# One-bank accumulator tiles for the seven-product pairs, and the two plain pairs finished in the down stage from DRAM

## The chip, the cores and the metric

The kernel runs on one core of a Trainium2 chip. The metric is the device time of one launch in microseconds (us): the median of three runs. A profile of one further execution says where that time goes. Engines are named as the profile names them: PE (TensorE, matmuls) with PEld (its weight loads), DVE (VectorE), ACT (ScalarE), POOL (GpSimd) and SP (SyncE, which here only issues DMAs).

## The reference, cut to what matters

One decoder layer for 1024 tokens of 1024 channels: a token-mixing half (dilated attention, a convolution module, gates) and then the channel-mixing half (FFN), which alone is changed:

```python
h = rms_norm(x, norm_ffn_pre)                         # 1024 x 1024
u = h @ w_up                                          # 1024 x 5632: 22 gate and 22 value columns of 128
u = causal_depthwise_conv(u, ffn_conv_w, ffn_conv_b)  # 3 taps along the tokens
u_gate, u_val = jnp.split(u, 2, axis=-1)
f = gelu(u_gate, approximate=True) * u_val            # 1024 x 2816
y = f @ w_down
x = x + rms_norm(y, norm_ffn_post)
```

All products are carried out in fp32 accuracy as three matmuls each, on operands split into a high part (`wh`, `xh`) and a low part (`wl`, `xl`): high by high, high by low, low by high.

## The kernel before, in words

**Where the FFN stands.** Attention, convolution and output projection come first and are not touched. From about 1125 us on the FFN's up stage computes, for each j from 0 to 21, a gate block and a value block of 128 channels by 1024 tokens. `us` is the name of such blocks in the plain pairs; in the trace all of them, and all other 128 by 1024 work tiles, are called `u` (six buffers).

**PSUM tiles.** There are eight banks of 128 by 512 fp32. `pp` is a tile of two banks with two buffers; `ps` is one bank with two buffers; `pt` and `po` are one bank with one buffer each. Dependencies between instructions are found by the Tile layer, tile by tile.

**The plain pairs** (`up_plain`, j = 0 and 1) do the full eight products of 12 matmuls each per pair: two columns c (gate and value), two token halves h, two halves kh of the inner dimension. Pair 0 sums into two `pp` tiles, one for each c, with the token halves side by side; pair 1 into `ps`, `ps`, `pt` and `po`. Each finished bank is copied to `us` (L731, by ACT for c = 0 and by DVE for c = 1). At the end `up_plain` finishes both pairs: scale and bias on ACT (`scaled`, L680), two taps on DVE (`taps`, L686), gelu on ACT (L736), product on DVE (L737), store to the DRAM buffer `fscr` by a POOL DMA (L738).

**The seven-product pairs** (class `Seven`, j = 2 to 21) need seven products P1 to P7 instead of eight. They use sums of weight quadrants made on POOL (L758) and sums T1 to T4 of the token operands, which DVE, ACT and POOL prepare during `up_plain` (L639, L640, L660 to L671). A pair has two accumulators, b1 and b2. P1, P2 and P3 add into b1, and P5, P6, P7 and P4 into b2; in between, `take` copies partial sums out, or from one accumulator to the other:

- after P5: b2 to the gate block (L774), then b1 over b2 (L775), both ACT
- after P2: b1 to the gate block (L777, ACT); after P6: b2 over b1 (L779, ACT)
- after P7 and P3: DVE adds of b2 (L782) and of b1 (L784) into the value and the gate block
- after P4: b2 to the value block (L786, ACT)

In the kernel before, b1 and b2 are the two banks of one `pp` tile, and successive pairs take its two buffers in turn.

**What sets the order.** For the seven-product pairs a table sets it: `AT` gives each product a place, seven places to a pair, and all steps of all pairs are sorted by place and rank and written out under a manual schedule. So PE runs, round and round, P2 and P6 of pair n, P1 of pair n + 1, P7 of n, P5 of n + 1, P3 and P4 of n. Weights are split (`wsplit`: L166 on ACT, L167 on DVE; seven buffers) five places ahead, scale, taps, gelu (L798), product (L804) and store (L807) of a pair follow at places 13 to 17. `up_plain` and the down stage are ordered by the scheduler, from their place in the code, and each engine works its own list strictly in order.

**The down stage** (`down(0)`, `down(1)`, one for each half of the tokens) loads block k of `fscr` by a POOL DMA (L858), splits it (L859 on ACT, L860 on DVE) and two weight pieces (L166, L167), and adds 24 matmuls into eight banks, two for each of four token tiles t. The last three k are done tile by tile, and `finish` (L838 to L849) normalises and writes a finished tile.

Of the kernel before, what the change touches and what calls it, by code (L numbers as in the profile page):

```python
# [11 lines left out]
F32 = mybir.dt.float32  # L12
# [6 lines left out]
P = 128  # L19
S = 1024  # L20
# [58 lines left out]
def trunk_kernel(ctx: ExitStack, tc: tile.TileContext, a, out):  # L79
# [9 lines left out]
    def pp_tile():  # L89
        return psum.tile([P, S], F32, tag="pp", name="pp", bufs=2)  # L90
# [3 lines left out]
    def ps_tile(shape=(P, 512), tag=None):  # L94

        if tag is None:
            tag = ("ps", "pt", "ps", "po")[banks[0] % 4]
            banks[0] += 1
        return psum.tile(list(shape), F32, tag=tag, name=tag, bufs=2 if tag == "ps" else 1)
# [574 lines left out]

    with tc.tile_pool(name="ffn", bufs=1) as ffn:
        fscr = dram.tile([NF, P, S], F32, name="fscr")

        def scaled(src, c):
            o = u_tile()
            nc.scalar.activation(o, src, AF.Identity, scale=ffn_w[:, c, 2:3], bias=ffn_b[:, c:c + 1])  # L680
            return o

        def taps(o, src, c):
            for k in (1, 0):
                d = 2 - k
                nc.vector.scalar_tensor_tensor(o[:, d:], src[:, :S - d], ffn_w[:, c, k:k + 1], o[:, d:],  # L686
                                               op0=ALU.mult, op1=ALU.add)
# [24 lines left out]
        def up_plain(js):  # L712

            us = {(j, c): u_tile() for j in js for c in range(2)}
            pps = [pp_tile() for c in range(2)]
            kept = {}
            for h in range(2):
                for n, j in enumerate(js):
                    for c in range(2):
                        ps = pps[c][:, h * 512:(h + 1) * 512] if n == 0 else ps_tile(tag=("ps", "ps", "pt", "po")[2 * h + c])  # L720
                        for kh in range(2):
                            key = j, 2 * c + kh
                            if h == 0 or key not in kept:
                                w = wsplit(quadrant(*key))
                                if len(kept) < 7:
                                    kept[key] = w
                            else:
                                w = kept[key]
                            product(ps, w, ("B11", "B21", "B12", "B22")[2 * h + kh], kh == 0, kh == 1)
                        dst = us[j, c][:, h * 512:(h + 1) * 512]  # L730
                        (nc.vector.tensor_copy if c else nc.scalar.copy)(dst, ps)  # L731
            for j in js:
                o = [scaled(us[j, c], c * NF + j) for c in range(2)]
                for c in range(2):
                    taps(o[c], us[j, c], c * NF + j)
                nc.scalar.activation(o[0], o[0], AF.Gelu_apprx_tanh)  # L736
                nc.vector.tensor_mul(o[0], o[0], o[1])  # L737
                nc.gpsimd.dma_start(fscr[j], o[0])  # L738

# [6 lines left out]
        class Seven:  # L748
# [13 lines left out]

            def multiply(self, p):
                if p == "P1":
                    both = pp_tile()
                    self.b1, self.b2 = both[:, 0:512], both[:, 512:1024]
                b = self.b1 if p in ("P1", "P2", "P3") else self.b2
                product(b, self.t[p], OPERAND[p], p in ("P1", "P5"), False, True)

# [81 lines left out]
        def down(h, late=3):  # L851
            wide = [pp_tile() for _ in range(2)]
            banks = [[w[:, cs] for cs in cols] for w in wide]
            banks += [[ps_tile(tag="ps") for _ in range(2)], [ps_tile(tag=tag) for tag in ("pt", "po")]]

            def load(k):
                ft = dt(F32R, (P, 2, 512))
                nc.gpsimd.dma_start(f(ft[:, 1]), fscr[k][:, h * 512:(h + 1) * 512])  # L858
                nc.scalar.copy(ft[:, 0], f(ft[:, 1]))  # L859
                nc.vector.tensor_sub(ft[:, 1], f(ft[:, 1]), f(ft[:, 0]))  # L860
                w = []
                for cs in cols:
                    raw = raw_tile()
                    nc.sync.dma_start(raw, a["w_down"][k * P:(k + 1) * P, cs])
                    w.append(wsplit(raw))
                return ft, w

            def step(t, k, ft, w):
                ts = slice(t * P, (t + 1) * P)
                for q in range(2):  # L870
                    mm3(banks[t][q], ft[:, 0, ts], ft[:, 1, ts], *w[q], k == 0, k == NF - 1)

            order = (3, 2, 0, 1)
            for k in range(NF - late):
                fw = load(k)
                for t in order:
                    step(t, k, *fw)
            fws = [(k, load(k)) for k in range(NF - late, NF)]
            for t in order:
                for k, fw in fws:  # L880
                    step(t, k, *fw)
                finish(4 * h + t, banks[t])
# [71 lines left out]
```

## Time and profile before

| | us |
|---|---|
| median of 3 runs (1868.88 to 1870.09) | 1869.4 |
| the profiled execution, device time | 1867.9 |
| its span, first to last instruction | 1866.1 |
| PE busy (95% of the span) | 1777.1 |
| DVE busy (63%) | 1170.3 |
| ACT busy (38%) | 717.4 |
| POOL busy (11%) | 206.0 |

All times from the trace are of the one profiled execution, counted from the start of its span. 1.8 us of its device time lie outside the span, and the median of the runs is 1.5 us above it. A row of the time line gives start, duration, engine, line, operation, output and inputs, shapes and a count where equal instructions are joined; in brackets stands how long the engine had been idle before, and what released it. Matmul rows overlap: a matmul's row lasts 0.39 us while the next starts after about 0.23. The granted clock is a share of TensorE's full 2.4 GHz, so 0.50 is its lower level, 1.2 GHz.

### The profile page before, as it was taken

Reading aid. Unit: us, or ns where it says so; the run is one execution under the profiler, and the core shown is the slowest. Engines: PE = TensorE matmul, PEld = TensorE weight load, DVE = VectorE, ACT = ScalarE, POOL = GpSimd, SP = SyncE. Lnnn points to the kernel's source line nnn. Section 1 sums busy time; section 2 is a strip of 40 time slices with the busy share of each in tenths; the row PEclk is TensorE's granted clock in tenths of the full one; section 3 lists DMA queues with packets and bytes.
Section 4 is the critical chain, followed back from the end, with each engine's and each line's share of the span. In section 5 each row is a group of like instructions: output and inputs, shape, how many; then the busy total and the mean of one; then the engine's idle time right before and its main releaser. Section 6 shows DMA issues by size and latency. Waiting matters only on the chain.

```text
span 1866.1 us, 22153 instructions
## 1 busy us (share of the span) xinstructions
PE 1777.1 (95%) x8152; PEld 1479.1 (79%) x8152; DVE 1170.3 (63%) x1971; ACT 717.4 (38%) x1327; POOL 206.0 (11%) x233
## 2 busy tenths in 40 slices
PE   7899998999999999999999999899999999999997
PEld 5688898888888888888888887677777777788886
DVE  6249979258762869738645578856655566753524
ACT  6132343233323342223432344545444454642322
POOL 0000010011100000000000002232232222120000
PEclk9899999999999999999999999899999999999999
DMA  5312132112312222344231432322232222573522
GB/s 189 108 49 60 45 97 81 45 58 62 95 52 53 68 68 80 102 172 147 92 112 57 142 108 90 96 91 79 85 98 88 86 79 91 180 249 126 173 93 100
DMA packets 83133, 184.01 MB, mean 99 GB/s; under 512 B 11203, under 2 KB 13139, under 8 KB 83024
## 3 DMA queue, kind: packets, MB, share of 16 engines
q1 hardware_dynamic: 67536, 139.75, 23.8%
q0 software_dynamic: 12240, 39.27, 6.5%
q10 hardware_dynamic: 3248, 3.58, 0.6%
q8 instruction: 64, 1.05, 0.2%
q14 instruction: 45, 0.37, 0.1%
HBM read 147.81 MB, written 36.85 MB: 99 GB/s over the span
## 4 chain that ended last, share of the span: by engine, by line
PE 61%; issue 28%; DVE 4%; POOL 2%; DMA 2%; ACT 1%; ACTq 1%; SPq 0%; POOLq 0%; DVEq 0%
PE pp L709 21%; PE pp L186 10%; PE pp L187 10%; PE pp L188 10%; PE ps L186 1%; PE ps L188 1%; PE ps L187 1%; DVE u L784 1%; ACTq L258 1%; ACT u L777 1%; POOL oscr L416 1%; POOL mscr L416 1%; PE pt L188 1%; PE po L188 1%; PE po L187 1%
## 5 line engine op out<-in xcount | busy, mean ns | idle before, releaser
L186 PE MATMUL pp<-d,wh 128*128 128x512 f32 x1088 | 428.0, 394 | 15.3 <-DVE d L332 15.0
L188 PE MATMUL pp<-d,wl 128*128 128x512 f32 x1088 | 427.4, 393 | 0.0
L187 PE MATMUL pp<-d,wh 128*128 128x512 f32 x1088 | 427.0, 393 | 0.0
L709 PE MATMUL pp<-d,wh 128*128 128x512 f32 x1184 | 375.3, 398 | 41.7 <-DVE u L784 17.0
L271 DVE SCALAR_TENSOR_TENSOR acc<-cin,conv_w,acc 128x1024 f32<-128x1024 f32 x240 | 305.2, 1281 | 3.1
L709 PEld LDWEIGHTS pp<-d,wh 128*128 128x128 f32 x1184 | 221.4, 190 | 104.0 <-DVE u L784 25.1
L186 PEld LDWEIGHTS pp<-d,wh 128*128 128x128 f32 x1088 | 205.1, 189 | 57.8 <-issue 16.0
L188 PEld LDWEIGHTS pp<-d,wl 128*128 128x128 f32 x1088 | 205.0, 188 | 41.3
L187 PEld LDWEIGHTS pp<-d,wh 128*128 128x128 f32 x1088 | 205.2, 189 | 40.8
L709 PE MATMUL pp<-d,wl 128*128 128x512 f32 x592 | 232.8, 393 | 0.0
L167 DVE TENSOR_TENSOR wl<-wr,wh 128x512 fp32r<-128x512 f32 x200 | 136.5, 687 | 152.5 <-ACT wh L166 152.0
L166 ACT CAST wh<-wr 128x512 fp32r<-128x512 f32 x200 | 123.3, 621 | 264.7 <-PE pp L187 166.5
L167 DVE TENSOR_TENSOR wl<-wq,wh 128x512 fp32r<-128x512 f32 x148 | 108.2, 740 | 99.7 <-ACT wh L166 97.1
L166 ACT CAST wh<-wq 128x512 fp32r<-128x512 f32 x148 | 91.1, 623 | 126.9 <-PE pp L188 104.7
L167 DVE TENSOR_TENSOR wl<-ws,wh 128x512 fp32r<-128x512 f32 x80 | 63.2, 790 | 113.1 <-ACT wh L166 113.1
L709 PEld LDWEIGHTS pp<-d,wl 128*128 128x128 f32 x592 | 112.4, 190 | 24.2
L686 DVE SCALAR_TENSOR_TENSOR u<-u,ffn_w 128x1023 f32<-128x1023 f32 x88 | 113.5, 1292 | 3.4 <-ACT u L680 2.0
L186 PE MATMUL pp<-wh,d 128*128 128x512 f32 x232 | 90.1, 391 | 0.7 <-ACT u L616 0.7
L187 PE MATMUL pp<-wl,d 128*128 128x512 f32 x232 | 90.4, 390 | 0.0
L188 PE MATMUL pp<-wh,d 128*128 128x512 f32 x232 | 90.4, 390 | 0.0
L325 PE MATMUL pp<-wh,d 128*128 128x512 f32 x192 | 79.1, 413 | 3.0 <-DVE d L332 3.0
L326 PE MATMUL pp<-wl,d 128*128 128x512 f32 x192 | 78.4, 408 | 0.0
(293 smaller groups left out, 2527.7 us busy)
## 6 DMA issues: line engine op xcount, KB each, us to landing
wq<-in_w_up_dram SPq DMA_DIRECT2D x100, 256.0 KB, 2.7
wq<-in_w_down_dram SPq DMA_DIRECT2D x88, 256.0 KB, 3.1
wr<-in_w_v_dram SPq DMA_DIRECT2D x48, 256.0 KB, 2.8
wr<-in_w_qk_dram SPq DMA_DIRECT2D x48, 256.0 KB, 2.7
fscr<-u POOLq DMA_DIRECT2D x22, 512.0 KB, 2.9
d<-fscr POOLq DMA_DIRECT2D x44, 256.0 KB, 5.2
wr<-in_w_glu_dram SPq DMA_DIRECT2D x32, 256.0 KB, 2.7
wr<-in_w_gate_dram SPq DMA_DIRECT2D x32, 256.0 KB, 2.7
```

The lines of the kernel that those rows point to most:

```text
L166: nc.scalar.copy(hi, raw)
L167: nc.vector.tensor_sub(lo, raw, f(hi))
L186: nc.tensor.matmul(ps, lh, rh, start=first, stop=False)
L187: nc.tensor.matmul(ps, lh, rl, start=False, stop=False)
L188: nc.tensor.matmul(ps, ll, rh, start=False, stop=last)
L258: nc.scalar.dma_start(bscr[4 * g:4 * g + 4, :, :BW[g]], vscr[4 * g:4 * g + 4, BOFF[g]:BOFF[g] + BW[g]].unsqueeze(1).to_broadcast((4, P, BW ...
L271: nc.vector.scalar_tensor_tensor(acc, cin[:, k:k + S], conv_w[:, m, k:k + 1], acc, op0=ALU.mult, op1=ALU.add)
L325: nc.tensor.matmul(ps, hTh[k][:, sl], wh, start=k == 0, stop=False)
L326: nc.tensor.matmul(ps, hTh[k][:, sl], wl, start=False, stop=False)
L416: nc.gpsimd.dma_start(dst[:, r, :, g, j, :], src[:, 2 * r:2 * r + 2, :])
L686: nc.vector.scalar_tensor_tensor(o[:, d:], src[:, :S - d], ffn_w[:, c, k:k + 1], o[:, d:], op0=ALU.mult, op1=ALU.add)
L709: nc.tensor.matmul(ps, wp[:, cs], xp, start=first and k == 0 and n == 0, stop=last and k == 3 and n == 2, skip_group_check=open_)
```

## The change

Two things are changed. First, b1 and b2 of a seven-product pair are two tiles of one bank each: `ps` and `ps` where j is even, `pt` and `po` where it is odd. Second, `up_plain` keeps pair 0 in one `pp` tile for each token half, copies all banks on ACT, after both columns are done, and then stores the raw blocks to a new DRAM buffer `uscr`. Scale, taps, gelu and product of the two plain pairs are a function of their own, `plain_out`, which loads them back. It is called in `down(0)`, after the fifth and the tenth k. So that `fscr[0]` and `fscr[1]` are wanted late, the down stage takes k from 2 to 21 and then 0 and 1, and its token tiles in the order 0 to 3.

```diff
--- before.py
+++ after.py
@@ -674,6 +674,7 @@
 
     with tc.tile_pool(name="ffn", bufs=1) as ffn:
         fscr = dram.tile([NF, P, S], F32, name="fscr")
+        uscr = dram.tile([2, 2, P, S], F32, name="uscr")
 
         def scaled(src, c):
             o = u_tile()
@@ -712,12 +713,15 @@
         def up_plain(js):
 
             us = {(j, c): u_tile() for j in js for c in range(2)}
-            pps = [pp_tile() for c in range(2)]
             kept = {}
             for h in range(2):
                 for n, j in enumerate(js):
-                    for c in range(2):
-                        ps = pps[c][:, h * 512:(h + 1) * 512] if n == 0 else ps_tile(tag=("ps", "ps", "pt", "po")[2 * h + c])
+                    if n == 0:
+                        both = pp_tile()
+                        pss = [both[:, 0:512], both[:, 512:1024]]
+                    else:
+                        pss = [ps_tile(tag=tag) for tag in (("ps", "ps"), ("pt", "po"))[h]]
+                    for c, ps in enumerate(pss):
                         for kh in range(2):
                             key = j, 2 * c + kh
                             if h == 0 or key not in kept:
@@ -727,15 +731,23 @@
                             else:
                                 w = kept[key]
                             product(ps, w, ("B11", "B21", "B12", "B22")[2 * h + kh], kh == 0, kh == 1)
-                        dst = us[j, c][:, h * 512:(h + 1) * 512]
-                        (nc.vector.tensor_copy if c else nc.scalar.copy)(dst, ps)
+                    for c, ps in enumerate(pss):
+                        nc.scalar.copy(us[j, c][:, h * 512:(h + 1) * 512], ps)
             for j in js:
-                o = [scaled(us[j, c], c * NF + j) for c in range(2)]
                 for c in range(2):
-                    taps(o[c], us[j, c], c * NF + j)
-                nc.scalar.activation(o[0], o[0], AF.Gelu_apprx_tanh)
-                nc.vector.tensor_mul(o[0], o[0], o[1])
-                nc.gpsimd.dma_start(fscr[j], o[0])
+                    nc.gpsimd.dma_start(uscr[j, c], us[j, c])
+
+        def plain_out(j):
+
+            o = []
+            for c in range(2):
+                u = u_tile()
+                nc.gpsimd.dma_start(u, uscr[j, c])
+                o.append(scaled(u, c * NF + j))
+                taps(o[c], u, c * NF + j)
+            nc.scalar.activation(o[0], o[0], AF.Gelu_apprx_tanh)
+            nc.vector.tensor_mul(o[0], o[0], o[1])
+            nc.gpsimd.dma_start(fscr[j], o[0])
 
 
 
@@ -762,8 +774,7 @@
 
             def multiply(self, p):
                 if p == "P1":
-                    both = pp_tile()
-                    self.b1, self.b2 = both[:, 0:512], both[:, 512:1024]
+                    self.b1, self.b2 = [ps_tile(tag=tag) for tag in (("ps", "ps"), ("pt", "po"))[self.j % 2]]
                 b = self.b1 if p in ("P1", "P2", "P3") else self.b2
                 product(b, self.t[p], OPERAND[p], p in ("P1", "P5"), False, True)
 
@@ -868,15 +879,17 @@
             def step(t, k, ft, w):
                 ts = slice(t * P, (t + 1) * P)
                 for q in range(2):
-                    mm3(banks[t][q], ft[:, 0, ts], ft[:, 1, ts], *w[q], k == 0, k == NF - 1)
-
-            order = (3, 2, 0, 1)
-            for k in range(NF - late):
+                    mm3(banks[t][q], ft[:, 0, ts], ft[:, 1, ts], *w[q], k == 2, k == 1)
+
+            ks = [*range(2, NF), 0, 1]
+            for n, k in enumerate(ks[:-late]):
                 fw = load(k)
-                for t in order:
+                for t in range(4):
                     step(t, k, *fw)
-            fws = [(k, load(k)) for k in range(NF - late, NF)]
-            for t in order:
+                if h == 0 and n in (4, 9):
+                    plain_out(n // 9)
+            fws = [(k, load(k)) for k in ks[-late:]]
+            for t in range(4):
                 for k, fw in fws:
                     step(t, k, *fw)
                 finish(4 * h + t, banks[t])
```

Three places of the engines' order, before and after (no times are in these rows; a wait is named by the engine or DMA queue whose semaphore is waited for). On PE, in the steady run of the seven-product pairs, the end of P2 and the start of P6 of pair 20. The first is written to b1, the second to b2. Before:

```order
L709 MATMUL pp_12176<-d168_8615,wl_12196 128x512
L709 MATMUL pp_12176<-d169_8616,wh_12195 128x512 x2
L709 MATMUL pp_12176<-d169_8616,wl_12196 128x512
L709 MATMUL pp_12176<-d186_9146,wh_12212 128x512 [waits Activation_49]
L709 MATMUL pp_12176<-d186_9146,wh_12212 128x512
L709 MATMUL pp_12176<-d186_9146,wl_12213 128x512
```

After:

```order
L710 MATMUL ps_12177<-d168_8615,wl_12198 128x512
L710 MATMUL ps_12177<-d169_8616,wh_12197 128x512 x2
L710 MATMUL ps_12177<-d169_8616,wl_12198 128x512
L710 MATMUL ps_12178<-d186_9146,wh_12214 128x512 x2
L710 MATMUL ps_12178<-d186_9146,wl_12215 128x512
L710 MATMUL ps_12178<-d187_9150,wh_12214 128x512 x2
```

P6 stood behind a wait for ACT and has none now; both products, and their place behind each other, are as they were. P4 behind P3 keeps a wait for DVE in both kernels.

On ACT, where the plain pairs end and the first `take` (the copies after P5 of pair 2) stands; the plain pairs' raw blocks are `u_9201` to `u_9204` before and `u_9202` to `u_9205` after (a wait for DMASW is one for a POOL DMA, here the store of `u_9202` to `uscr`). Before:

```order
L680 ACTIVATE u_9465<-u_9201,ffn_b_80,ffn_w_79 128x1024 [waits DVE_49]
L680 ACTIVATE u_9467<-u_9202,ffn_b_80,ffn_w_79 128x1024 [waits DVE_49]
L736 ACT_TABLE_LOAD [waits DVE_49]
L736 ACTIVATE u_9465<-u_9465 128x1024 [waits Activation_49]
L680 ACTIVATE u_9476<-u_9203,ffn_b_80,ffn_w_79 128x1024
L680 ACTIVATE u_9478<-u_9204,ffn_b_80,ffn_w_79 128x1024 [waits DVE_49,Activation_49]
L774 COPY u_9558<-pp_9511 128x512 [waits DVE_49,PE_49]
L775 COPY pp_9511<-pp_9511 128x512 [waits Activation_49]
```

After:

```order
L639 CAST d195_9184<-u_9123 128x512 [waits DVE_49]
L639 CAST d196_9189<-u_9124 128x512 [waits DVE_49]
L735 COPY u_9205<-po_9409 128x512 [waits PE_49]
L639 CAST d197_9194<-u_9124 128x512 [waits DVE_49,Activation_49]
L842 DMA d198_12513<-in_norm_ffn_post_dram 128x1024 [waits Activation_49]
L785 COPY u_9542<-ps_9495 128x512 [waits DMASW5_49,PE_49,Activation_49]
L786 COPY ps_9495<-ps_9494 128x512 [waits Activation_49]
```

The four scalings, the gelu and its table load of the plain pairs are gone from ahead of the first `take`, whose copies now follow the last casts of the operand sums and a bank copy.

On DVE, at the start of the down stage, behind the taps of the last pair, 21 (`u_12497` before, `u_12500` after); `u_12723`, `u_12729` and `u_12938` are blocks of the plain pairs. Before:

```order
L686 SCALAR_TENSOR_TENSOR u_12502<-u_12470,ffn_w_79,u_12502 128x1023 [waits Activation_49]
L686 SCALAR_TENSOR_TENSOR u_12502<-u_12470,ffn_w_79,u_12502 128x1022 [waits DVE_49]
L167 TENSOR_TENSOR wl_12651<-wq_12648,wh_12650 128x512 [waits DMAHW5_49,Activation_49]
L167 TENSOR_TENSOR wl_12685<-wq_12682,wh_12684 128x512 [waits DMAHW6_49,Activation_49]
L167 TENSOR_TENSOR wl_12691<-wq_12688,wh_12690 128x512 [waits DMAHW7_49,Activation_49]
L804 TENSOR_TENSOR u_12497<-u_12497,u_12502 128x1024 [waits DVE_49]
L167 TENSOR_TENSOR wl_12725<-wq_12722,wh_12724 128x512 [waits DMAHW0_49,Activation_49]
L167 TENSOR_TENSOR wl_12731<-wq_12728,wh_12730 128x512 [waits DMAHW2_49,Activation_49]
L167 TENSOR_TENSOR wl_12765<-wq_12762,wh_12764 128x512 [waits DMAHW3_49,Activation_49]
L167 TENSOR_TENSOR wl_12771<-wq_12768,wh_12770 128x512 [waits DMAHW4_49,Activation_49]
```

After:

```order
L815 TENSOR_TENSOR u_12500<-u_12500,u_12505 128x1024 [waits DVE_49]
L687 SCALAR_TENSOR_TENSOR u_12723<-u_12721,ffn_w_79,u_12723 128x1023 [waits DMASW7_49,DMASW5_49,Activation_49]
L167 TENSOR_TENSOR wl_12694<-wq_12691,wh_12693 128x512 [waits DMAHW7_49,Activation_49]
L167 TENSOR_TENSOR wl_12743<-wq_12740,wh_12742 128x512 [waits DMAHW0_49,Activation_49]
L167 TENSOR_TENSOR wl_12749<-wq_12746,wh_12748 128x512 [waits DMAHW1_49,Activation_49]
L167 TENSOR_TENSOR wl_12783<-wq_12780,wh_12782 128x512 [waits DMAHW2_49,Activation_49]
L687 SCALAR_TENSOR_TENSOR u_12723<-u_12721,ffn_w_79,u_12723 128x1022 [waits DVE_49]
L687 SCALAR_TENSOR_TENSOR u_12729<-u_12727,ffn_w_79,u_12729 128x1023 [waits DMASW0_49,Activation_49]
L167 TENSOR_TENSOR wl_12789<-wq_12786,wh_12788 128x512 [waits DMAHW3_49,Activation_49]
L687 SCALAR_TENSOR_TENSOR u_12729<-u_12727,ffn_w_79,u_12729 128x1022 [waits DVE_49]
L687 SCALAR_TENSOR_TENSOR u_12938<-u_12936,ffn_w_79,u_12938 128x1023 [waits DMASW2_49,DMASW1_49,Activation_49]
L749 TENSOR_TENSOR u_12723<-u_12723,u_12729 128x1024 [waits DVE_49,Activation_49]
```

The taps and the product of the plain pairs now stand between the weight splits (L167) of the down stage; ACT's scalings and gelus, and POOL's four loads and two stores, stand likewise among those of the down stage.

## Rows read from the trace of the kernel before

**Rows 1.** Windows: us, busy PE, PEld, DVE, ACT, POOL (count), clock, DMA share, GB/s.
```profile
1125.00:1185.50 60.50, 56.09 (x248) 45.29 (x246) 53.65 (x99) 30.38 (x58) 17.98 (x12) 0.94 0.26 83
...
1214.30:1573.50 359.20, 334.35 (x1428) 265.39 (x1428) 216.12 (x241) 172.62 (x256) 97.35 (x87) 1.00 0.28 88
1573.50:1607.70 34.20, 29.90 (x120) 23.54 (x121) 22.12 (x27) 20.29 (x32) 10.01 (x18) 0.95 0.41 132
...
1627.00:1855.40 228.40, 228.40 (x1008) 188.87 (x1006) 101.50 (x209) 79.13 (x143) 12.84 (x24) 1.00 0.44 145
1855.40:1866.10 10.70, 0.01 (x1) 0.00 (x0) 7.45 (x29) 2.03 (x5) 0.00 (x0) 0.61 0.42 158
```

**Rows 2.** Waits of PE from 1214 to 1574: total us, times, longest.
```profile
PE pp L709 <- DVE u L784: 14.1, 18, 0.8
PE pp L709 <- ACT u L777: 11.5, 17, 0.7
```

**Rows 3.** Time line of PE in one round of the seven-product pairs.
```profile
1541.25 0.62 PE L709 MATMUL pp<-d,wh 128*128 128x512 f32 x2
...
1550.77 0.62 PE L709 MATMUL pp<-d,wh 128*128 128x512 f32 x2
1551.22 0.39 PE L709 MATMUL pp<-d,wl 128*128 128x512 f32 x1
1552.40 0.74 PE L709 MATMUL pp<-d,wh 128*128 128x512 f32 x2 [0.78 <-DVE u L784]
...
1558.85 0.73 PE L709 MATMUL pp<-d,wh 128*128 128x512 f32 x2 [0.68 <-ACT u L777]
```

**Rows 4.** Time lines of DVE (first row) and ACT in the same round.
```profile
1557.24 2.60 DVE L686 SCALAR_TENSOR_TENSOR u<-u,ffn_w 128x1023 f32<-128x1023 f32 x2
...
1558.21 0.58 ACT L777 COPY u<-pp 128x512 f32<-128x512 f32 x1 [0.47 <-PE pp L709]
...
1559.87 1.06 ACT L798 ACTIVATE u<-u 128x1024 f32<-128x1024 f32 x1 [0.56 <-DVE u L686]
1561.96 0.57 ACT L779 COPY pp<-pp 128x512 f32<-128x512 f32 x1 [1.03 <-PE pp L709]
```

**Rows 5.** Time line of PE at the plain pairs and the first seven-product pair.
```profile
1152.65 1.22 PE L709 MATMUL pp<-d,wh 128*128 128x512 f32 x2 [2.97 <-DVE u L731]
...
1193.45 1.22 PE L709 MATMUL pp<-d,wh 128*128 128x512 f32 x2 [8.09 <-ACT pp L775]
...
1194.89 1.05 PE L709 MATMUL pp<-d,wh 128*128 128x512 f32 x2
...
1196.17 1.05 PE L709 MATMUL pp<-d,wh 128*128 128x512 f32 x2
```

**Rows 6.** Time lines of DVE (first row) and ACT behind the plain pairs.
```profile
1183.52 5.10 DVE L686 SCALAR_TENSOR_TENSOR u<-u,ffn_w 128x1023 f32<-128x1023 f32 x4
...
1188.44 2.36 ACT L680 ACTIVATE u<-u,ffn_b,ffn_w 128x1024 f32<-128x1024 f32 x2
1192.21 0.59 ACT L774 COPY u<-pp 128x512 f32<-128x512 f32 x1 [1.41 <-DVE u L737]
```

**Rows 7.** Time lines of POOL, DVE and PE where the down stage's loads begin.
```profile
1583.98 2.58 POOL L858 DMA_DIRECT2D d<-fscr  x4 [8.09 <-PE pp L709]
...
1596.06 0.68 DVE L784 TENSOR_TENSOR u<-pp,u 128x512 f32<-128x512 f32 x1
...
1596.80 0.73 PE L709 MATMUL pp<-d,wh 128*128 128x512 f32 x2 [2.92 <-DVE u L784]
```

**Rows 8.** The page's DMA issues: count, KB each, median us to landing.
```profile
fscr<-u POOLq DMA_DIRECT2D x22, 512.0 KB, 2.9
d<-fscr POOLq DMA_DIRECT2D x44, 256.0 KB, 5.2
```

**Rows 9.** Time lines of ACT and DVE behind the last matmul.
```profile
1855.44 0.58 ACT L838 COPY u<-pp 128x512 f32<-128x512 f32 x1 [1.74 <-PE pp L188]
...
1856.06 0.69 DVE L839 COPY u<-pp 128x512 f32<-128x512 f32 x1
```

## The prediction

> **What bounds the kernel now.** I read the windows by stage first [rows 1]. From 1627.0 to 1855.4 us, in the down stage, PE is busy in all of 228.40 us: 1008 matmuls, 0.2266 us each, and nothing but fewer or faster matmuls could shorten it. The seven-product stretch from 1214.3 to 1573.5 is not like that: 1428 matmuls (17 rounds of 84) take 359.20 us, 0.2515 each, at a granted clock of 1.00. DVE is busy for 60% of it, ACT for 48%, POOL for 27%, so no other engine is the bound. Then I read the list of waits for the same stretch [rows 2]: PE waits for two lines only, 18 times for DVE's L784 and 17 times for ACT's L777, once each in a round. The time line of a round shows them [rows 3]: P4 starts 0.78 us late behind the add that empties b1 after P3, and P6 0.68 us late behind the copy that empties b1 after P2. Both products write b2, the other bank of the same tile. They are waits for a tile, not for data. That is where to look in the rows: the releaser reads a bank that the waiting product does not write.
>
> How fast does a round run where nothing stops it? From 1541.25 to 1550.77 there are 14 groups of three matmuls [rows 3]: 9.52 / 42 = 0.2267 us each, the same as in the down stage. I take it for the rest.
>
> **The change part by part.** All terms are made against the profiled execution, 1867.9 us.
>
> (a) Steady rounds. 1428 x 0.2267 = 323.7 us, so the stretch loses 359.2 - 323.7 = 35.5 us, 2.09 a round. That is more than the listed waits (14.1 + 11.5 = 25.6): a matmul that starts late also gives up its overlap with the one before, as 1551.22 + 0.23 = 1551.45 against 1552.40 shows (0.95 us for a listed 0.78), and the first few after it run a little slower [rows 3]. With a tile for each bank the order's rows have no wait ahead of P6. P4 keeps one for DVE, but what it must wait for is the add after P7 (L782), which reads b2 and stands two products earlier. So the whole 35.5 goes, if nothing else is late. What is late next? P7 writes b2 after the copy L779, which stands on ACT behind the gelu of the pair before, and that behind DVE's taps. In the round shown the gelu ends at 1559.87 + 1.06 = 1560.93 [rows 4]. Without its wait P6 would start at 1558.85 - 0.83 = 1558.02 and end 2.72 later, at 1560.74; the copy takes 0.57 [rows 4], so it is done by about 1561.7 with the passing on. P1 of the next pair runs meanwhile, to 1563.46, and only then is P7 due: 1.8 us to spare. Taken: 35.5, bounds 25 (half a microsecond a round comes back) and 35.5.
>
> *The Trainium skill, page "PSUM — Partial Sum Buffer", section "PSUM bank collisions raise a hardware error", has it that engines must be kept apart by bank (and quarter of the partitions), and that different banks may be used at once. By it, nothing on the chip asks for the waits in rows 2, and the sum is as in (a); were two neighbouring banks barred together, (a) would be 0. No row of before has PE and ACT on the two banks of one pair at once, so the trace doesn't yet say.*
>
> (b) The first pair. In before, P2 of pair 2 starts 8.09 us late [rows 5], since the copies L774 and L775 stand on ACT behind the plain pairs' scalings and gelu, and those behind DVE's taps and product [rows 6]. Then 12 matmuls run at half the clock: 1.28 us for three [rows 5], 0.427 each, which costs 12 x 0.20 = 2.4. With the two ordinary waits of that round (2.09) and 0.2 of overlap, 12.8 us are lost between P5's end and P4. The order shows the scalings and the gelu gone from there. What stays: P2 must wait for the two copies after P5, 0.59 [rows 6] and about 0.57, and some 0.3 for passing on, 1.5 us. The first copy also waits for the store of a raw block to `uscr` to land, since it takes over its buffer; such a store takes 2.9 us [rows 8], its block is copied out some 11 us (pair 1's last products, P1 and P5) before P5 ends, so it is hidden; if it isn't, it costs a few us once. Gain 11.3, bounds 7 and 12.8.
>
> (c) The plain pairs. PE waits 2.97 us for DVE's copy L731 and then runs 12 matmuls at half the clock (2.4) [rows 5]: 5.4 us. Now no copy is on DVE, and the second half goes to another `pp` tile. But DVE's operand sums set the pace there (53.65 of 60.50 us busy [rows 1]), the next operands' casts stand on ACT behind three copies of about 0.5 us, and transposes and short waits stay. Half of it stays, I estimate: gain 2.5, bounds 0 and 5.4.
>
> (d) The end of the pairs. From 1573.5 to 1607.7 120 matmuls take 34.2 us where 27.2 would do [rows 1]: 7.0 lost, in three ordinary waits and one of 2.92 us at P4 of pair 20, behind DVE's L784 [rows 7]. DVE and ACT were held by splits of down-stage blocks, whose loads start at 1583.98 [rows 7] and take 5.2 us to land [rows 8]. In the new order P4 no longer waits for L784, and the add it does wait for ends about a microsecond before P4 is due. But the first down-stage matmuls come earlier, and their weight splits stand on DVE behind the same blocks and the taps of pair 20: I work out from the rows' durations that they are late by some 2 to 3 us, with a few matmuls at half the clock behind. Gain 3.5, bounds 0 and 7.
>
> (e) The end. The last tile is now `pt` and `po`, not one `pp`: DVE's copy need not follow ACT's (1856.06 after 1855.44 + 0.58 [rows 9]). Gain 0.6.
>
> (f) What is added. Four raw stores, four loads, and the finishing of two pairs in the down stage. On DVE that is 8 taps of 1.28 (5.10 / 4 [rows 6]) and 2 products of about 1.2: 12.6 us; on ACT 4 scalings of 1.2 and 2 gelus of 1.06 [rows 4, 6]: 7 us. PE covers it: in its 228.40 us DVE has 127 free and ACT 149 [rows 1], and the weight splits that are queued behind run up to seven buffers, three and a half k (19 us of PE), ahead. A raw block's way is load, scale, taps, gelu, product, store, load: about 5 + 1 + 3 + 1 + 1 + 3 + 5 = 19 us, and blocks 0 and 1 are wanted after 18 others of 5.4 us each. POOL's queue holds only loads and stores by then. Cost 0. If the cover fails at the two places where ACT waits for a raw block, each costs a load's 5 to 6 us: bound 12.
>
> Sum: 35.5 + 11.3 + 2.5 + 3.5 + 0.6 = 53.4, so 1867.9 - 53.4 = 1814.5. The median of the runs lies 1.5 us above the profiled execution: **1816.0**.
>
> **The rivals.** *A new wait in each round.* The 1.8 us to spare at P7 is the smallest I found. If a faster PE makes ACT's line (sums on POOL, split, scale, taps, gelu, copy) late by more, each microsecond beyond it costs 20 us. For it: the chain passes through three engines that work strictly in order. Against it: all three are idle 40% or more of a round, and the chain starts from PE's own products. Half a microsecond to 1.2 a round: 1826 to 1840.
>
> *The change does not do what it says:* the two waits stay, because P4's and P6's partner copies must be over for another reason, a bank rule or a count that the semaphore passes late. Then (a) is nothing, and (b) to (e) leave about 17 us, less the waits in them: 1853. For it: P4 keeps a wait for DVE. Against it: P6 has none for ACT.
>
> *The down stage doesn't cover* the moved work (f): up to 12 us back, 1828.
>
> *Slower:* the clock. Without its pauses PE works on for some 400 us in the pairs; if the chip then granted 1.2 GHz for part of it, each matmul would take 0.427 instead of 0.227 [rows 3, 5]. 268 of the 1680 (16%) would eat the 53.4 us, and half of them at that level would end at 1867.9 - 53.4 + 168 = 1982 us. Against it: 228.40 us without a pause at clock 1.00 [rows 1]; for it, only that the half clock occurs at all, and each time here behind a pause of about 3 us or more [rows 5].
>
> *The Trainium skill, page "TensorE: Matmul & The Clock Gate", Part 1, has the low clock as the default, which activity lifts: by it steady work can't bring this rival about. The trace agrees in rows 1 and 5.*
>
> **How the numbers follow.** The forecast as worked out: 0.82. A new wait in each round 0.08, the waits stay 0.03, the down stage doesn't cover 0.04, the clock 0.03. Within the forecast the bounds of (b) to (d) give at best 35.5 + 12.8 + 5.4 + 7 + 0.6 = 61.3 (1808), and at worst 35.5 + 7 + 0 + 0 + 0.6 = 43.1 (1826). All three at one end at once is unlikely; I take 1809 to 1828, which holds nearly all of the forecast, the down-stage case and the lower edge of the new wait, and leaves out about 0.14. A measurement of this kernel can tell about 0.2% (4 us) from no change. Faster by more than that: 0.96; within it 0.01; slower 0.03.
>
> **What the profile would show.** (a) right: a stretch of 17 rounds takes about 324 us, without a wait ahead of P4 or P6; wrong, if PE waits for L790 (the new copy after P6) or for a split. (b): P2 of the first pair waits 1 to 2 us, not 8. (c): no wait for a copy among the plain pairs, but small ones for operands. (d): some 2 to 3 us of waiting for a split where the down stage starts. (f): PE without a pause from there to its end; a wait there for L166, L167 or L870 would show the moved work uncovered. The forecast is wrong as a whole if rounds still take over 20 us.

## The result, and the profile after

The changed kernel takes 1818.4 us (median of four runs, 1814.4 to 1822.7), the kernel before 1869.7 (1868.9 to 1870.3). The ratio is 0.9726, with a 95% interval of 0.9703 to 0.975: 51 us saved. Forecast were 1816.0 and a range of 1809 to 1828. The profiled execution of the changed kernel is the longest of its four: 1822.7, with a span of 1820.6.

The first thing to read is where the FFN begins, since nothing ahead of it was changed. The rows of L616, a copy in the output projection some 70 us ahead of it, give count, shortest, median and longest duration in ns, then the first and the last start. Before:

```profile
L616 ACT COPY u<-pp x14: 585/590/608, 1054.5 to 1114.6; 128x512 f32<-128x512 f32 x14
```

After:

```profile
L616 ACT COPY u<-pp x14: 587/591/609, 1061.1 to 1121.2; 128x512 f32<-128x512 f32 x14
```

The same work comes 6.6 us later in the profiled execution of after. So the stretches must be set side by side from there, not by their times. Windows of after (us, then busy PE, PEld, DVE, ACT and POOL with counts, granted clock, DMA share, GB/s):

```profile
1131.60:1188.35 56.75, 53.29 (x248) 43.41 (x246) 48.33 (x93) 30.50 (x60) 23.39 (x15) 1.00 0.30 98
1188.35:1206.05 17.70, 16.43 (x72) 13.63 (x73) 7.55 (x9) 8.32 (x15) 7.22 (x6) 1.00 0.53 164
1206.05:1529.75 323.70, 323.70 (x1429) 268.02 (x1428) 228.92 (x241) 175.50 (x259) 99.59 (x88) 1.00 0.33 100
1529.75:1556.95 27.20, 27.20 (x121) 22.34 (x119) 20.08 (x25) 18.71 (x29) 10.94 (x18) 1.00 0.49 155
1556.95:1580.10 23.15, 21.36 (x87) 17.15 (x86) 18.35 (x25) 12.02 (x20) 2.48 (x5) 0.93 0.58 195
1580.10:1808.50 228.40, 228.40 (x1008) 188.81 (x1006) 111.18 (x220) 84.97 (x148) 16.07 (x30) 1.00 0.47 157
1808.50:1820.60 12.10, 0.01 (x1) 0.00 (x0) 8.22 (x29) 1.92 (x5) 0.00 (x0) 0.58 0.55 188
```

[rows 1] holds the answering rows of before for five of these; two stretches of before were not among them:

```profile
1185.50:1214.35 28.85, 19.41 (x72) 14.98 (x72) 21.13 (x22) 15.09 (x23) 9.76 (x9) 0.82 0.30 101
...
1607.70:1627.00 19.30, 19.30 (x87) 15.96 (x86) 14.47 (x22) 9.60 (x16) 2.49 (x5) 1.00 0.68 225
```

| stretch | before | after | change | forecast |
|---|---|---|---|---|
| up to the first copy of L616 | 1054.5 | 1061.1 | +6.6 | 0 |
| plain pairs, to the end of P5 (c) | 60.5 | 56.8 | -3.7 | -2.5 |
| first pair, to its P4 (b) | 28.9 | 17.7 | -11.2 | -11.3 |
| 17 steady rounds (a) | 359.2 | 323.7 | -35.5 | -35.5 |
| end of the pairs and start of the down stage (d) | 34.2 + 19.3 | 27.2 + 23.2 | -3.1 | -3.5 |
| rest of the down stage, with the added work (f) | 228.4 | 228.4 | 0.0 | 0 |
| behind the last matmul (e) | 10.7 | 12.1 | +1.4 | -0.6 |

The whole list of PE's waits in the changed part (us, times, longest) has three rows now, where [rows 2] alone held 35 waits:

```profile
PE pp L710 <- DVE d L640: 3.4, 2, 2.3
PE pp L187 <- DVE wl L167: 1.8, 1, 1.8
PE ps L710 <- ACT ps L786: 1.3, 1, 1.3
```

One steady round of after, first PE's rows where P6 and P7 start (start, duration, engine, line, operation, tiles, shape, count), then ACT's:

```profile
1420.96 0.62 PE L710 MATMUL ps<-d,wh 128*128 128x512 f32 x2
...
1426.40 0.62 PE L710 MATMUL ps<-d,wh 128*128 128x512 f32 x2
```

```profile
1421.16 0.59 ACT L788 COPY u<-ps 128x512 f32<-128x512 f32 x1 [0.47 <-PE ps L710]
...
1422.82 1.06 ACT L809 ACTIVATE u<-u 128x1024 f32<-128x1024 f32 x1 [0.55 <-DVE u L687]
1423.93 0.57 ACT L790 COPY ps<-ps 128x512 f32<-128x512 f32 x1
```

P6 begins at 1420.96, right behind P2, while ACT copies b1 from 1421.16 to 1421.75. In [rows 3, 4] P6 began only when that copy was over. L790, on which P7 depends, ends at 1423.93 + 0.57 = 1424.50, and P7 is due at 1426.40: 1.9 us to spare, 1.8 were forecast.

*The Trainium skill, page "PSUM — Partial Sum Buffer", section "PSUM bank collisions raise a hardware error", lets two engines use different banks at once. The trace agrees here: P6 writes one ps bank in the 0.59 us in which ACT reads the other, and its matmuls keep their step.*

Where the down stage starts, PE's rows and then DVE's:

```profile
1559.96 0.50 PE L187 MATMUL pp<-wl,d 128*128 128x512 f32 x1 [1.79 <-DVE wl L167]
...
1561.99 0.63 PE L188 MATMUL ps<-wh,d 128*128 128x512 f32 x1
```

```profile
1554.91 2.60 DVE L687 SCALAR_TENSOR_TENSOR u<-u,ffn_w 128x1023 f32<-128x1023 f32 x2
...
1558.03 1.28 DVE L687 SCALAR_TENSOR_TENSOR u<-u,ffn_w 128x1023 f32<-128x1023 f32 x1
1559.22 1.89 DVE L167 TENSOR_TENSOR wl<-wq,wh 128x512 fp32r<-128x512 f32 x3
```

The split for which PE waits stands behind the taps of pair 20, as forecast, and 1.6 us behind the pause eight matmuls run at 0.427 us each, the half clock (1.2 GHz). Both together make most of the 3.9 us that this start costs in this execution.

### The profile page after: what moved, and what is told of

Read it like the earlier page. It is cut to its first block, busy times and chain, and to the rows that moved or that the text cites. A ratio compares the mean times of both kernels' runs of the same rounds, so it can differ in the third digit from the quotient of the medians.

```text
span 1820.6 us, 22184 instructions
## 1 busy us (share of the span) xinstructions
PE 1767.3 (97%) x8152; PEld 1483.4 (81%) x8152; DVE 1177.1 (65%) x1967; ACT 720.7 (40%) x1331; POOL 215.4 (12%) x241
## 4 chain that ended last, share of the span: by engine, by line
PE 61%; issue 29%; DVE 3%; POOL 3%; DMA 2%; ACT 1%; ACTq 1%; SPq 0%; POOLq 0%; DVEq 0%
PE ps L710 10%; PE pp L186 10%; PE pp L187 10%; PE pp L188 10%; PE po L710 6%; PE pt L710 4%; PE ps L188 1%; PE ps L187 1%; PE ps L186 1%; PE pp L710 1%; POOL oscr L416 1%; ACTq L258 1%; POOL mscr L416 1%; PE po L188 1%; PE pt L188 1%
## 5 line engine op out<-in xcount | busy, mean ns | idle before, releaser
L186 PE MATMUL pp<-d,wh 128*128 128x512 f32 x1088 | 430.0, 396 | 15.1 <-DVE d L332 14.8
L188 PE MATMUL pp<-d,wl 128*128 128x512 f32 x1088 | 428.9, 394 | 0.0
L187 PE MATMUL pp<-d,wh 128*128 128x512 f32 x1088 | 428.7, 394 | 0.0
L186 PEld LDWEIGHTS pp<-d,wh 128*128 128x128 f32 x1088 | 206.2, 189 | 58.0 <-issue 15.7
L188 PEld LDWEIGHTS pp<-d,wl 128*128 128x128 f32 x1088 | 206.1, 189 | 41.7
L187 PEld LDWEIGHTS pp<-d,wh 128*128 128x128 f32 x1088 | 206.3, 190 | 41.2
L167 DVE TENSOR_TENSOR wl<-wr,wh 128x512 fp32r<-128x512 f32 x200 | 136.9, 689 | 153.8 <-ACT wh L166 152.7
L710 PE MATMUL ps<-d,wh 128*128 128x512 f32 x592 | 182.6, 389 | 1.3 <-ACT ps L786 1.3
L167 DVE TENSOR_TENSOR wl<-wq,wh 128x512 fp32r<-128x512 f32 x148 | 119.3, 814 | 93.5 <-ACT wh L166 93.5
L710 PEld LDWEIGHTS ps<-d,wh 128*128 128x128 f32 x592 | 111.1, 188 | 24.8 <-ACT ps L786 1.7
L167 DVE TENSOR_TENSOR wl<-ws,wh 128x512 fp32r<-128x512 f32 x80 | 63.7, 799 | 81.6 <-ACT wh L166 81.6
L710 PE MATMUL ps<-d,wl 128*128 128x512 f32 x296 | 115.3, 389 | 0.0
L710 PE MATMUL po<-d,wh 128*128 128x512 f32 x336 | 103.6, 389 | 0.0
```

Of the source, the lines that this page charges most:

```text
L167: nc.vector.tensor_sub(lo, raw, f(hi))
L186: nc.tensor.matmul(ps, lh, rh, start=first, stop=False)
L187: nc.tensor.matmul(ps, lh, rl, start=False, stop=False)
L188: nc.tensor.matmul(ps, ll, rh, start=False, stop=last)
L710: nc.tensor.matmul(ps, wp[:, cs], xp, start=first and k == 0 and n == 0, stop=last and k == 3 and n == 2, skip_group_check=open_)
```

## The experiments

Eight kernels ran. The kernel before took 1870.0 us (seven runs) beside the first four and 1870.2 (13 other runs) beside the last four.

### The changed kernel again

> The changed kernel once more, nothing altered. Theory A: of the 1820.6 us of the profiled execution some 6.6 us were lost before the changed part begins, because three pauses of 3 us at L332 were followed by matmuls at the half clock in that execution and not in the one of before; that is chance from one execution to the next. Then the median lies again between 1814 and 1823, the first copy of L616 (1054.5 us in before, 1061.1 in after) starts somewhere between 1054 and 1063, and the whole time moves with it. Rival: the change itself slows the part in front of it; then L616 starts at 1061 again, within 1 us.

Measured: 1818.0 us (1817.5 to 1818.8), profiled span 1815.4. Its row of L616, and the matmuls behind the third pause, with that pause's row of before and of after ahead:

```profile
L616 ACT COPY u<-pp x14: 586/591/611, 1058.2 to 1118.3; 128x512 f32<-128x512 f32 x14
```

Before:

```profile
537.95 0.47 PE L186 MATMUL pp<-d,wh 128*128 128x512 f32 x1 [2.98 <-DVE d L332]
538.26 0.39 PE L187 MATMUL pp<-d,wh 128*128 128x512 f32 x1
```

After:

```profile
541.70 0.77 PE L186 MATMUL pp<-d,wh 128*128 128x512 f32 x1 [3.03 <-DVE d L332]
...
542.69 0.63 PE L188 MATMUL pp<-d,wl 128*128 128x512 f32 x1
```

The same wait of 3.0 us is followed by matmuls every 0.23 us in one execution and every 0.43 us, for 14 matmuls, in the other. L616 starts at 1058.2 this time. In the six other kernels that leave this part alone it starts at 1054.5 (before), 1057.5 (tiles alone), 1061.9 (move alone), 1056.6 (without the finishing), 1058.5 and 1057.0 (two and six copies added). So it moves within 7.4 us, by 2.9 for one and the same kernel, and theory A holds. The profiled execution of before is at the low end: by its trace no matmul at all ran at the half clock behind those three pauses. That before also starts as late as 1061 in some executions is not shown, as it was profiled once.

The start of the down stage moves too. PE waits there again, but the clock is 1.00 behind the wait, and the start costs 1.9 us in place of 3.9:

```profile
1556.38 0.50 PE L187 MATMUL pp<-wl,d 128*128 128x512 f32 x1 [1.59 <-DVE wl L167]
```

From the first copy of L616 to the end this execution is 54.4 us shorter than the one of before; the first one of the changed kernel was 52.1 shorter.

### The one-bank tiles alone

```diff
-                    both = pp_tile()
-                    self.b1, self.b2 = both[:, 0:512], both[:, 512:1024]
+                    self.b1, self.b2 = [ps_tile(tag=tag) for tag in (("ps", "ps"), ("pt", "po"))[self.j % 2]]
```

> The kernel before with one edit: the two accumulators of a seven-product pair are one-bank tiles. The plain pairs stay as they were. Theory A (the two waits of a round are for the two-bank tile): 17 rounds give back 35.5 us, the rounds at the two ends another 4 to 6, the 8.1 us wait of the first pair stays, and the down stage, whose first tile is now pt and po that the last pair has just left, starts 1 to 2 us late: 1869.7 - 40 + 1.5, about 1831. Rival (the chip or a semaphore count asks for the waits, and the gain came from the plain pairs' move): 1869.

Measured: 1826.8 us (1824.6 to 1829.1), ratio 0.977 (0.9755 to 0.9784), 43.3 us less than before. PE's window of 280 us in the steady rounds (busy, count, clock, DMA share, GB/s), and its waits from 1190 to 1600:

```profile
1220.00:1500.00 280.00, 280.00 (x1237) 1.00 0.32 99
```

```profile
PE ps L709 <- ACT ps L774: 9.1, 1, 9.1
PE ps L187 <- DVE wl L167: 1.4, 1, 1.4
```

Not one wait is left in the rounds. PE and ACT, or PE and DVE, still use the two accumulators at once; only the tile that held both is gone. That settles it against the rival that the chip, or a count that a semaphore passes late, asks for the waits. (Whether the two banks lie side by side, as those of a `pp` tile do, no view shows.) The sum was 4 us too careful at the ends: 35.5 for the steady rounds, 2.9 for the first, 7.0 at the end, less 1.7 at the start of the down stage (the wait of 1.4 and what it takes along), make 43.7.

### The move of the plain pairs alone

```diff
-                    self.b1, self.b2 = [ps_tile(tag=tag) for tag in (("ps", "ps"), ("pt", "po"))[self.j % 2]]
+                    both = pp_tile()
+                    self.b1, self.b2 = both[:, 0:512], both[:, 512:1024]
```

(against the changed kernel)

> The changed kernel with the old two-bank tile for the accumulators: what is left is the move of the plain pairs' taps and gelu to the down stage and the copies on ACT. Theory A: the rounds take 21.13 us again, the first pair's long wait is gone (about 9 us back, with its half clock), the plain pairs give 2.5 to 4: 1869.7 - 12.5, about 1857, range 1853 to 1860. Rival (the two parts need each other, since in the old rounds the added copies on ACT come on the path): 1865 or more.

Measured: 1859.0 us (1857.8 to 1863.5), ratio 0.9946 (0.9931 to 0.9962), 11.0 less than before. PE's waits from 1200 to 1580:

```profile
PE pp L710 <- DVE u L796: 14.1, 18, 0.8
PE pp L710 <- ACT u L789: 12.2, 18, 0.7
```

The old pair of waits is back [rows 2], to a tenth of a microsecond for DVE and with one wait more for ACT, so that theory A holds here too. The two parts give 43.3 + 11.0 = 54.3 alone and 52.0 together. Where the missing 2.3 us lie is not shown: at the start of the down stage tiles alone lose 1.7 us, and both together 3.9 in one trace and 1.9 in the other.

### Without the added work

```diff
-                for c in range(2):
-                    nc.gpsimd.dma_start(uscr[j, c], us[j, c])
+                nc.gpsimd.dma_start(fscr[j], us[j, 0])
...
-                if h == 0 and n in (4, 9):
-                    plain_out(n // 9)
```

> The changed kernel without the added work in the down stage: the raw blocks of the plain pairs aren't stored and read back, and their scaling, taps, gelu and product are left out; one raw block of each pair goes straight to where the finished block belongs. Theory A (the work lies wholly beside PE's matmuls): the same time as the changed kernel, 1814 to 1822. Rival (the down stage doesn't cover it): up to 12 us less, 1806.

Measured: 1817.1 us (1815.7 to 1818.4), 0.9 below the changed kernel beside it. A window of 228.4 us that ends just behind the last matmul (by 1.5 and 1.1 us), without the work and then (the changed kernel again) with it, same columns as the windows of after:

```profile
1575.00:1803.40 228.40, 226.87 (x1001) 187.55 (x1000) 100.23 (x213) 76.80 (x141) 13.90 (x26) 1.00 0.44 145
```

```profile
1576.00:1804.40 228.40, 227.29 (x1003) 187.92 (x1001) 112.11 (x222) 84.10 (x147) 16.01 (x30) 1.00 0.48 157
```

DVE has 11.9 us less to do and ACT 7.3 (12.6 and 7 were forecast), and the stage is no shorter: from the last product of the pairs to the last matmul it is 230.9 us in both. The added work is hidden; a bound of 12 us is narrowed to about 1, which is within the spread of the runs.

### Where the slack of a round ends

Two and six copies are put behind the gelu, ahead of the copy on which P7 depends (below with two):

```diff
                 nc.scalar.activation(self.og, self.og, AF.Gelu_apprx_tanh)
+                for _ in range(2):
+                    nc.scalar.copy(self.og[:, 0:512], self.og[:, 0:512])
```

> The changed kernel with two more copies of 128x512 (about 0.6 us each, a block onto itself) on ACT behind each pair's gelu, ahead of the copy L790 on which P7 depends: 1.2 us a pair. Theory A (in the steady round L790 ends 1.8 us ahead of P7): nothing, 1816 to 1821. Rival (the line through ACT is already the pace, so that each added microsecond shows): 20 x 1.2 = 24 us more, 1842.

> The same with six such copies, about 3.6 us a pair. Theory A: 1.8 us of it goes into the slack, the other 1.8 us is a wait of PE ahead of P7 in each of 20 rounds, some 36 us and a little for each restart: 1854, range 1845 to 1862. Rival 1 (the line through ACT is already the pace): 72 us, 1890. Rival 2 (the slack is much larger than read): 1818.

With two: 1820.1 us (1818.4 to 1822.8). ACT's rows and the start of P7:

```profile
1421.42 1.28 ACT L811 COPY u<-u 128x512 f32<-128x512 f32 x2
1422.60 0.58 ACT L790 COPY ps<-ps 128x512 f32<-128x512 f32 x1
```

```profile
1423.90 0.62 PE L710 MATMUL ps<-d,wh 128*128 128x512 f32 x2
```

L790 ends at 1423.18, 0.7 us ahead of P7. No wait appears. The median is 2 us up, as much as the changed kernel's own runs differ.

With six: 1869.7 us (1865.0 to 1871.1), as slow as the kernel before. ACT's copies, then PE where P7 starts in three rounds, with a row behind the second start:

```profile
1410.03 3.89 ACT L811 COPY u<-u 128x512 f32<-128x512 f32 x6
```

```profile
1240.70 0.73 PE L710 MATMUL ps<-d,wh 128*128 128x512 f32 x2 [1.78 <-ACT ps L790]
...
1261.83 0.73 PE L710 MATMUL po<-d,wh 128*128 128x512 f32 x2 [1.77 <-ACT pt L790]
...
1264.75 1.06 PE L710 MATMUL po<-d,wh 128*128 128x512 f32 x2
...
1284.56 0.73 PE L710 MATMUL ps<-d,wh 128*128 128x512 f32 x2 [1.77 <-ACT ps L790]
...
1305.67 0.73 PE L710 MATMUL po<-d,wh 128*128 128x512 f32 x2 [1.77 <-ACT pt L790]
```

The mechanism is theory A's: 3.8 us added, 1.9 of slack, and a pause of 1.78 ahead of P7. The size was off by 16 us. A round takes 21.11 us (1284.56 to 1305.67) where it took 19.04, so 2.07 a round, and in every second or third round 22.73 (1261.83 to 1284.56): behind that pause eight matmuls ran at the half clock, which costs 1.6 us. From 1217.97 to 1565.53 there are 16 rounds, and six of them are of the long kind. The pause is the same in both kinds. With the first and the last there are 18 pauses, eight of them with the half clock behind: 18 times 2.07 and eight times 1.6 make 50 of the 51 us, and the first and the last pause are longer, 2.5 and 2.8 us.

### The same edit in a stage that the change left alone

```diff
-                    pv = [pp_tile() for _ in range(2)]
+                    if half == 0:
+                        pv = [w[:, h * 512:h * 512 + 512] for w in (pp_tile(), pp_tile()) for h in range(2)]
+                    else:
+                        pv = [ps_tile(tag=tag) for tag in ("ps", "ps", "pt", "po")]
...
-                            ps = pv[t4 // 2][:, (t4 % 2) * 512:(t4 % 2) * 512 + 512]
+                            ps = pv[t4]
```

> The changed kernel with the same kind of edit in a stage that the change did not touch: the second half of the value projection accumulates in four one-bank tiles (ps, ps, pt, po) in place of two two-bank tiles, so that neither it nor the stage behind it waits for the four evictions of a half. Theory A: three waits of 3.0 us at L332 go (9 us), and with them the matmuls at half clock that follow them in some executions (0 to 7 us), so that the runs also lie closer together: 1818 - 9 - 3 = 1806, range 1802 to 1810, spread of the runs 4 us or less. Rival (the spread comes from elsewhere): 1809, and the runs still spread over 5 us or more.

Measured: 1787.9 us (1787.2 to 1789.7), ratio 0.9563 (0.9549 to 0.9577) against the kernel before; 30 us better than the changed kernel, so it beats both. PE's windows in this kernel (busy, count, clock, DMA share, GB/s):

```profile
60.00:130.00 70.00, 70.00 (x340) 1.00 0.30 85
250.00:360.00 110.00, 108.93 (x530) 1.00 0.29 84
500.00:600.00 100.00, 100.00 (x485) 1.00 0.23 65
```

The changed kernel's windows, and its waits from 60 to 1000:

```profile
60.00:130.00 70.00, 61.22 (x283) 0.95 0.27 76
250.00:360.00 110.00, 104.70 (x474) 0.94 0.25 73
500.00:600.00 100.00, 93.95 (x418) 0.95 0.21 57
```

```profile
PE pp L186 <- DVE d L332: 14.8, 3, 8.8
PE pp L325 <- DVE d L332: 3.0, 1, 3.0
PE po L399 <- DVE ost L404: 2.4, 1, 2.4
```

The waits at L332 are gone, 0.7 us is left of the one at L399, and the clock is 1.00 in all three windows. The gain was forecast as 12 and measured as 30, for two reasons that the rows show. I had counted the three waits of 3.0 us and left out the first of 8.8, since the splits of weights ahead of it wait for DMAs; it is listed for the same evictions, and it went with them, as did most of the 2.4 us at L399: 19.5 us and not 9. And the clock was granted at 0.95, 0.94 and 0.95 in these windows, which by these shares is 3.5 + 6.6 + 5.0, about 15 us, where I took 3. The two can't simply be added, since the clock is low in a part of the pauses too: it is 0.50 from 76.6 to 80.2, the end of the first one, where PE stands still. The FFN's first matmul starts at 1098.3, 33.5 us earlier than in the trace of after and 30.5 earlier than in the changed kernel again. Between theory A and its rival the waits decide, not the time, which lies below both. Nor does the spread: these runs lie within 2.5 us, but the four of the changed kernel again lay within 1.3.

### The end of the kernel

```diff
-            xr = u_tile()
+            xr = dt()
```

(in `finish`, on top of the edit before)

> The kernel of v1 with one edit more: the residual block of the last stage's finish lies in a tile of the other pool, so that the six u buffers are not used up by three output tiles. Theory A: the copies out of the last tile wait in the changed kernel for a buffer whose rows are still being stored; without that they start 0.2 us behind the last matmul and not 1.7, and the end comes 1.5 us sooner: 1.5 us less than v1. Rival (DVE's queue, not the buffer, holds the end): the time from the last matmul to the end stays at 12.1 us.

Measured: 1788.9 us (1787.6 to 1790.0), no different from the 1787.9 without it. ACT's copy of the last tile without the edit, and then ACT's and DVE's copies with it:

```profile
1775.33 0.58 ACT L852 COPY u<-pt 128x512 f32<-128x512 f32 x1 [4.08 <-DVE u L862]
```

```profile
1773.79 0.59 ACT L852 COPY u<-pt 128x512 f32<-128x512 f32 x1 [1.95 <-PE pt L188]
1774.46 0.69 DVE L853 COPY u<-po 128x512 f32<-128x512 f32 x1 [0.20 <-PE po L188]
```

The last matmul ends at 1773.85 without the edit and at 1774.43 with it. The copies start 1.5 us behind it without, and with it at once, so the wait was for the buffer, as theory A has it. But from the last matmul to the end it is 11.4 us in place of 12.1: only 0.7 is gained. By the trace DVE now works off the normalisation of the three last tiles in one queue; no run tested that. Both theories were half right.

## Why the prediction was right, and where it was not

**(a) Steady rounds: right, to 0.1 us.** 323.7 us were forecast from 1428 matmuls of 0.2267, and 323.7 is what the window shows, without a wait ahead of P4 or P6. Three things were needed. The releaser of each wait read a bank that the waiting product does not write [rows 2, 3], which pointed to the tile; one-bank tiles alone took all of it away. The price came from the step of undisturbed matmuls and not from the listed waits: the list had 25.6 us, the gain was 35.5. And what would be late next was worked out; the 1.8 us of slack forecast were 1.9, and the two kernels with added copies found its end between 1.3 and 3.8 us.

**(b) The first pair: right.** 11.2 for 11.3. P2 waits 1.3 us for the two copies, where 1.5 were said to stay.

**(c) The plain pairs: right in kind, 1.2 us too small.** The wait for DVE's copy is gone and waits for operands took its place, as forecast (L640, 3.4 us). What makes it better than forecast is the clock, and that is in part luck: behind a pause of 2.35 us it was 1.00 in this execution, against 0.94 before [rows 1]. With the six copies added, which do not touch this stretch, the same pause of 2.35 us was followed by matmuls at the half clock, and the stretch took 2.4 us more.

**(d) The end of the pairs: right in kind.** All 7.0 come back, and a part is lost again at the start of the down stage, at the weight split that the text named. That the gain of 3.1 comes so near to 3.5 is in part luck: 3.9 are lost where the half clock follows the wait, as in this execution, and 1.9 where it doesn't, as in the second one, whose gain is 5.1.

**(e) The end: wrong by 2.0 us, in sign too.** The step that failed looked at one engine: DVE's copy need not follow ACT's, and it does not (1810.03 and 1810.05). But the change also turned the order of the token tiles round, and with it the last copies found their `u` buffer still in use: ACT's row has a wait of 4.10 us for L859 there.

```profile
1810.03 0.59 ACT L849 COPY u<-pt 128x512 f32<-128x512 f32 x1 [4.10 <-DVE u L859]
```

A step that is moved meets other buffers, and those should have been followed through as the PSUM tiles were. The two parts alone bear it out: behind the last matmul lie 10.7 us with the one-bank tiles and the old order, and 12.1 with the move and the new order. Why the order of tiles makes DVE reach the third last tile's result later was read from the trace only; no run turned the order alone back.

**(f) The added work: right.** Nothing, by the window and by the kernel without it. (The 18 blocks ahead of 0 and 1 are twenty by the new order, and ten from the later call of `plain_out` on; at 5.4 us each that is still more than the 19 us needed.)

**The level.** The terms sum to 53.4, and the stretches show 52.1 in one execution of the changed kernel and 54.4 in the other. I set the sum against one execution of before and added 1.5 us for its median; that execution was one in which the three pauses at L332 cost no clock, and other executions lose up to 7 us there. This was in no term. So the mechanism was right, but that the median lies only 2.4 us from the forecast is in part luck: single executions of the changed kernel lie between 1814.4 and 1822.7, and what decides which it is lies outside the sum.

**The rivals.** A new wait in each round did not come; six added copies a round bring it about, with a price near 50 us. That the change would not do what it says is excluded by the tiles alone. The down stage covers the moved work. The clock stayed at 1.00 for 323.7 us and again for 228.4 without a pause, so steady work did not lower it.

## What to carry to other kernels

When PE waits for an engine that reads a bank which the waiting product does not write, the wait belongs to the tile: look for tiles of two banks wherever evictions and products alternate, as the value projection gave another 30 us by the same edit. Price such waits by counting undisturbed matmuls, not by adding up the listed waits, and then follow what is late next through every buffer that the edit moves. Compare two traces only from a row that both share just ahead of the change.

## What the runs showed of the hardware that was not expected

The half clock (1.2 GHz) does not need a pause of 3 us, as the prediction had it. The trace of before already shows otherwise: the clock was 0.51 from 294.4 to 297.8, shortly behind a pause of 2.35 us at L399, and 1.00 behind the three of 2.9 to 3.0 us at L332. With six copies added it came behind six of 16 pauses of 1.78 us, for eight matmuls and 1.6 us each time, at every second or third one, and not behind the other ten. At the start of the down stage it came behind a wait of 1.79 us in after, and not behind the same wait in the kernel without the added work:

```profile
1554.92 0.50 PE L187 MATMUL pp<-wl,d 128*128 128x512 f32 x1 [1.79 <-DVE wl L167]
```

Behind the 35 pauses of 0.7 to 0.8 us of the old rounds the clock was 1.00 [rows 1, 2]. So in these traces a pause of about 2 to 3 us costs its length, or its length and another 1.5 to 3 us, and its length does not tell which. Two executions of the changed kernel differ by 5.2 us in their spans: 2.9 ahead of L616 and 2.0 at the start of the down stage, both at places where the half clock came in different measure.

*The Trainium skill, page "TensorE: Matmul & The Clock Gate", Part 1, has it that the number of slow matmuls varies from run to run, with the moment at which work begins. The runs agree on the number: behind the second pause at L332, 2.9 us long, 14 matmuls were slow in after, eight in the changed kernel again and none in before. What decides it no run here shows.*
